# A two-layer encoder trunk: no GpSimd work on tiles, full inputs kept for the seven-product sums, and seven products in the first feed-forward layer from its eleventh tile on

## The chip, the cores and the metric

The kernel runs on one core of one Trainium2 chip. The core has TensorE (PE, matrix products; PEld is its weight loads), VectorE (DVE), ScalarE (ACT), GpSimd (POOL) and SyncE (SP), which here issues every transfer. The metric is the device time of one launch in microseconds. Before the change it is 2225.82 us, the median of three runs (2225.81 to 2229.15).

## The reference

512 tokens of width 1024 pass two layers of three residual blocks. Each block's input is modulated by a condition vector c, and each block ends in a layer norm:

```
for i in range(2):
    mods = (silu(c) @ ada_w[i] + ada_b[i]).reshape(b, 3, 3, 1024)      # shift, scale, gate of each block
    y = swiglu(modulate(x, mods[:, 0]), w_gate, w_up, w_down)          # width 2816
    x = layer_norm(ALPHA * x + 0.5 * gate(0) * y, g, b)
    u = modulate(x, mods[:, 1])
    y = mamba2_bidir(u, ...) if i == 0 else diff_attention(u, ...)
    x = layer_norm(ALPHA * x + gate(1) * y, g, b)
    y = swiglu(modulate(x, mods[:, 2]), w_gate, w_up, w_down)
    x = layer_norm(ALPHA * x + 0.5 * gate(2) * y, g, b)
def swiglu(u, w_gate, w_up, w_down): return (silu(u @ w_gate) * (u @ w_up)) @ w_down
```

All of it is float32. A modulation by `mods` follows each layer norm, so the kernel folds the two into one scale and one bias per channel.

## The kernel before

Activations lie transposed: 1024 channels are eight tiles (KT) of 128 partitions by 512 tokens. The residual `res` holds eight such tiles for the whole run. A float32 product is made from rounded high and low parts, with three matmuls (`mm3`, L158 to L166: high-high, high-low, low-high). A weight block of 512 KB lands in a ring of four `raw` buffers; ScalarE rounds it to its high part (L119 `wh`) and VectorE subtracts to get the low part (L120 `wl`). The first blocks of each stage go into tiles of the activation pool instead, in halves of 512 columns (`wah` L110, `wal` L112), and every first half's low part is made by GpSimd.

The stages by number n are: 0 feed-forward, 1 state-space mixer, 2 and 3 feed-forward, 4 attention, 5 feed-forward. Each ends in a layer norm LN0 to LN5. In the profiled execution they lie roughly so: FFN0 from 11 to 352 us, LN0 to 405, mixer to 806, LN1 to 850, FFN2 to 1166, LN2 to 1213, FFN3 to 1533, LN3 to 1573, attention to 1829, LN4 to 1866, FFN5 to 2178, LN5 to 2226.

A feed-forward stage (`ffn`, L507) runs 22 pairs of gate and up tiles in parts of 8, 7 and 7, and after each part its down projection, eight units (`down_units`) of one 128-channel output tile each. A standard pair takes 2 x 24 matmuls of 512 columns. From tile `first7` on a pair is made by `seven` (L476): seven products of half-size blocks instead of eight, with sums of weight blocks (`weight_forms`, L454 to L464) and sums of input halves (`input_forms`, L424), which are made over the four tiles before `first7`. FFN2, FFN3 and FFN5 have `first7=4`; FFN0 has 22, so it has no such tile, though its forms are made at tiles 18 to 21.

The modulation vectors are a product of weights with the condition, made by VectorE from blocks of 512 KB (`ada_unit`, L180). `ada_stream` is a list of such units; `advance(stream, k)` puts k of them into the program at that place. `per` says how many: its first number for a standard tile, its second for a unit of the down projection of parts 0 and 1. FFN0 has (3, 0), FFN2 and FFN3 (1, 2).

The last down projection of a stage holds the layer norm. Its first units run on all 512 tokens, the last ones (four, in some stages six) on each half of the tokens in turn, so that the first half's statistics can be made while the second half is computed. `LN.start` subtracts the channel-tile mean (L272 matmul, L274 copy, L277 eight subtractions, of which GpSimd does the last two). `feed` adds up the values (`sc`, L292) and their squares (`ss`, L293), on GpSimd except at the end. `stats` makes the mean and variance with matmuls (L299, L303), takes the power on GpSimd (L317), and spreads it by matmuls (L249). `normalize` multiplies (L347), writes the next input's high part `uh` and a temporary full-precision copy `lt` with ScalarE (L349), and the low part `ul` with VectorE (L350). L371 adds a down-projection result to the residual.

The order of instructions on each engine is fixed when the kernel is built: a scheduler places them by program order, by readiness and by when tiles of the pools come free. Tiles with the tag `a` (the activation pool: `hi`, `lo`, `wah`, `wal` and others) share NA = 32 buffers, and are handed out in the order of the program's requests.

Of the kernel before, what the change touches and what calls it, by code (L numbers as in the profile page):

```python
# [9 lines left out]
F32 = mybir.dt.float32  # L10
F32R = mybir.dt.float32r
AF = mybir.ActivationFunctionType
# [5 lines left out]
KT = D // P  # L18
FT = 22
FPARTS = (8, 7, 7)  # L20
NA = 32
NE = 5
NG = 4
NST = 128
# [22 lines left out]
def hybrid_trunk(tc, xT, cb, par, cst, adaw, wgu, wdn0, wdn1, wdn2, wdt, win, wso, wqk, wv, wao, dist_in, dtp, lam_in, out):  # L47
# [17 lines left out]
    def tmp(name="tmp"):  # L65
        return tp.tile([P, T], F32, tag="t", name=name)
# [28 lines left out]

    extra = [None]
    behind = []
    first_split = [True]
    first_ln = [None]
    turn = [0]  # L100

    def split(raw, where=None):

        n = raw.shape[-1]
        if where == "a":
            hi, lo = [], []
            for o in range(0, n, T):
                r = raw[:, o : o + T]
                h, l = big(F32R, "wah"), big(F32R, "wal")
                x = nc.scalar.activation(h, r, AF.Copy)  # L110
                eng = nc.vector if first_split[0] or o else nc.gpsimd
                y = eng.tensor_tensor(out=l, in0=r, in1=h.bitcast(F32), op=ALU.subtract)  # L112
                for a, b in zip((x, y), behind):
                    tc.add_manual_dep(a.ins, b.ins.name, NOSYNC, reason="inputs before weights")
                hi.append(h)
                lo.append(l)
            return [(hi[c // T][:, c % T : c % T + P], lo[c // T][:, c % T : c % T + P]) for c in range(0, n, P)]
        hi, lo = ring()
        nc.scalar.activation(hi[:, :n], raw, AF.Copy)  # L119
        nc.vector.tensor_tensor(out=lo[:, :n], in0=raw, in1=hi[:, :n].bitcast(F32), op=ALU.subtract)  # L120
        return Unit(hi, lo, n)
# [138 lines left out]
    class LN:  # L260
# [6 lines left out]
        def start(self):  # L267

            pm = acc("ln")
            z0 = tp.tile([P, T], F32R, tag="t", name="z0")  # L270
            nc.scalar.activation(z0, res[0], AF.Copy)
            nc.tensor.matmul(pm, lhsT=onesn, rhs=z0, start=True, stop=True)  # L272
            m0 = ap.tile([P, T], F32, tag="l", name="m0", bufs=3)
            nc.scalar.activation(m0, pm, AF.Copy)  # L274
            for d in range(KT):
                eng = nc.gpsimd if d >= 6 else nc.vector
                eng.tensor_tensor(out=res[d], in0=res[d], in1=m0, op=ALU.subtract)  # L277
# [3 lines left out]
        def feed(self, d, a, b, late=False):  # L281
# [11 lines left out]
            e1.tensor_tensor(out=self.ss[:, a:b], in0=self.ss[:, a:b], in1=sq[:, a:b], op=ALU.add)  # L293

        def stats(self, a, b):
            n, m = self.n, (b - a) // P
# [27 lines left out]
        def normalize(self, a, b, rb):  # L324
# [14 lines left out]
            if self.u is None:  # L339
                self.u = [  # L340
                    tuple(ap.tile([P, T], F32R, tag="u", name=x, bufs=2 * KT) for x in ("uh", "ul")) for _ in range(KT)
                ]
            for d in range(KT):
                G, B = lnG[n][:, d : d + 1], lnB[n][:, d : d + 1]
                z, t = res[d][:, a:b], tmp("lt")[:, a:b]
                uh, ul = self.u[d][0][:, a:b], self.u[d][1][:, a:b]
                nc.vector.tensor_tensor(out=z, in0=z, in1=rb, op=ALU.mult)  # L347
                for o in (uh, t):
                    nc.scalar.activation(o, z, AF.Identity, bias=B, scale=G)  # L349
                nc.vector.tensor_tensor(out=ul, in0=t, in1=uh.bitcast(F32), op=ALU.subtract)  # L350
# [22 lines left out]
            op0=ALU.mult, op1=ALU.add,  # L373
        )

    next_u = [None]

    def first_units(n):

# [8 lines left out]
    def down_units(n, u, units, last, KEEP=4):  # L388
# [15 lines left out]
        if last:  # L404
            rbs = []
            for a, b in HALVES:
                for d, w in keep:
                    pd = acc()
                    proj(pd, w, u, cols=((a, b),))
                    add_res(d, pd, n, a, b)  # L410
                    ln.feed(d, a, b, late=True)
# [11 lines left out]

    def input_forms(u):

        for k in range(4):
            top, bot = tmp("ft"), tmp("fb")
            for o, d in ((top, k), (bot, k + 4)):  # L430
                nc.vector.tensor_tensor(out=o, in0=u[d][0].bitcast(F32), in1=u[d][1].bitcast(F32), op=ALU.add)
# [72 lines left out]
        hs.append(split_act(sg))  # L504


    def ffn(n, stream=None, per=(0, 0), pre=None, first7=FT):  # L507
# [6 lines left out]
        u = next_u[0]  # L514
        f = 0
        pre = pre or first_units(n)
        for pi, nf in enumerate(FPARTS):
            hs = []
            open7 = None
            for _ in range(nf):  # L520
# [19 lines left out]
                nc.vector.tensor_tensor(out=h, in0=sg, in1=pu, op=ALU.mult)  # L540
                hs.append(split_act(h))
                if first7 - 4 <= f < first7:
                    making = making or input_forms(u)
# [490 lines left out]
    for d in range(KT):  # L1034
# [20 lines left out]
    first_split[0] = False  # L1055
# [114 lines left out]
```

## Time and profile before

| what | value |
|---|---|
| median of 3 runs | 2225.82 us (2225.81 to 2229.15) |
| profiled execution | 2227.95 us, span 2226.2 us |
| granted TensorE clock, mean | 0.991 |
| PE busy | 2161.8 us (97%) |
| DVE busy | 1697.3 us (76%) |
| ACT busy | 1055.2 us (47%) |
| POOL busy | 273.4 us (12%) |
| read from memory | 289.5 MB |

Busy times are of one execution. In a row of a group the count follows the x, then come busy time and mean duration in ns; the last column says how long the engine stood idle before and what released it. Where a row has three durations with slashes they are the shortest, the median and the longest, and the two times behind them are the first and the last start. In the rows of the timeline the first number is the start and the second the duration in us. A matmul's duration is longer than the distance to the next one, since matmuls overlap.

### The profile page before, as it was taken

Reading aid. Unit: us, or ns where it says so; the run is one execution under the profiler, and the core shown is the slowest. Engines: PE = TensorE matmul, PEld = TensorE weight load, DVE = VectorE, ACT = ScalarE, POOL = GpSimd, SP = SyncE. Lnnn points to the kernel's source line nnn. Section 1 sums busy time; section 2 is a strip of 40 time slices with the busy share of each in tenths; the row PEclk is TensorE's granted clock in tenths of the full one; section 3 lists DMA queues with packets and bytes.
Section 4 is the critical chain, followed back from the end, with each engine's and each line's share of the span. In section 5 each row is a group of like instructions: output and inputs, shape, how many; then the busy total and the mean of one; then the engine's idle time right before and its main releaser. Section 6 shows DMA issues by size and latency. Waiting matters only on the chain.

```text
span 2226.2 us, 33653 instructions
## 1 busy us (share of the span) xinstructions
PE 2161.8 (97%) x13030; PEld 1862.6 (84%) x13030; DVE 1697.3 (76%) x2850; ACT 1055.2 (47%) x1758; POOL 273.4 (12%) x332
## 2 busy tenths in 40 slices
PE   7999999999999989999999999999999999999998
PEld 5788888866777679889898989899877778989897
DVE  6865568556766689989888998897766679959696
ACT  4422234757656537434355534344755556425253
POOL 2000003035332330000003000003000012000003
PEclk9999999999999999999999999999999999999999
DMA  8865562375445423545542273733211122323231
GB/s 300 283 210 175 181 200 80 96 184 150 136 132 156 119 70 107 193 156 184 166 133 92 92 253 103 238 106 122 68 57 52 53 67 67 115 75 116 84 117 46
DMA packets 88545, 296.97 MB, mean 133 GB/s; under 512 B 9536, under 2 KB 12992, under 8 KB 88384
## 3 DMA queue, kind: packets, MB, share of 16 engines
q1 hardware_dynamic: 88384, 294.81, 41.8%
q8 instruction: 102, 1.67, 0.3%
q14 instruction: 59, 0.48, 0.1%
HBM read 289.53 MB, written 5.24 MB: 132 GB/s over the span
## 4 chain that ended last, share of the span: by engine, by line
PE 48%; DVE 9%; issue 4%; ACT 3%; DMA 2%; POOL 1%; POOLq 0%; ACTq 0%; DVEq 0%; SPq 0%
PE acc L162 38%; PE mid L162 6%; DVE wl L120 1%; DMA raw<-in_wdn 1%; PE mid L938 1%; DVE raw L464 1%; PE ln L162 1%; DVE wl L455 1%; DVE raw L180 1%; DVE lo L150 1%; PE ln L249 1%; DMA raw<-in_adaw 1%; ACT wh L119 1%; DVE resid L277 1%; DVE resid L371 0%
## 5 line engine op out<-in xcount | busy, mean ns | idle before, releaser
L162 PE MATMUL acc<-hi,wh 128*128 128x512 f32 (+1 forms) x1488 | 506.0, 341 | 9.8 <-DVE resid L371 6.7
L162 PE MATMUL acc<-hi,wl 128*128 128x512 f32 (+1 forms) x1488 | 505.9, 340 | 1.1 <-DVE wl L455 1.1
L162 PE MATMUL acc<-lo,wh 128*128 128x512 f32 (+1 forms) x1488 | 504.9, 339 | 0.0
L162 PE MATMUL acc<-uh,wh 128*128 128x512 f32 (+1 forms) x1256 | 441.6, 352 | 0.3 <-ACT wh L119 0.3
L162 PE MATMUL acc<-ul,wh 128*128 128x512 f32 (+1 forms) x1256 | 439.5, 350 | 0.2 <-DVE ul L1047 0.2
L162 PE MATMUL acc<-uh,wl 128*128 128x512 f32 (+1 forms) x1256 | 438.2, 349 | 0.8 <-DVE wl L120 0.8
L119 ACT ACTIVATE wh<-raw 128x1024 fp32r<-128x1024 f32 (+1 forms) x234 | 238.6, 1025 | 392.3 <-PE acc L162 199.1
L120 DVE TENSOR_TENSOR wl<-raw,wh 128x1024 fp32r<-128x1024 f32 (+1 forms) x234 | 281.2, 1202 | 81.1 <-ACT wh L119 71.3
L162 PEld LDWEIGHTS acc<-hi,wh 128*128 128x128 f32 x1488 | 283.8, 191 | 46.2 <-DVE resid L371 6.5
L162 PEld LDWEIGHTS acc<-hi,wl 128*128 128x128 f32 x1488 | 284.1, 191 | 32.2 <-DVE wl L455 1.5
L162 PEld LDWEIGHTS acc<-lo,wh 128*128 128x128 f32 x1488 | 283.9, 191 | 31.0 <-DVE lo L150 1.0
L162 PEld LDWEIGHTS acc<-uh,wh 128*128 128x128 f32 x1256 | 237.4, 189 | 40.2 <-issue 9.2
L454 ACT ACTIVATE wh<-raw 128x1024 fp32r<-128x1024 f32 x162 | 170.8, 1059 | 207.5 <-DVE raw L464 105.2
L162 PEld LDWEIGHTS acc<-uh,wl 128*128 128x128 f32 x1256 | 237.6, 189 | 35.0 <-issue 3.9
L162 PEld LDWEIGHTS acc<-ul,wh 128*128 128x128 f32 x1256 | 237.8, 189 | 33.7 <-issue 4.4
L180 DVE SCALAR_TENSOR_TENSOR raw<-raw,cond 128x1024 f32<-128x1024 f32 x144 | 176.9, 1235 | 55.8 <-DMA raw<-in_adaw 55.4
L455 DVE TENSOR_TENSOR wl<-raw,wh 128x1024 fp32r<-128x1024 f32 x162 | 196.9, 1219 | 27.1 <-ACT wh L454 26.1
L371 DVE SCALAR_TENSOR_TENSOR resid<-acc,gv,resid 128x512 f32<-128x512 f32 (+1 forms) x172 | 113.0, 659 | 78.5 <-PE acc L162 78.2
L464 DVE TENSOR_TENSOR raw<-raw 128x512 f32<-128x512 f32 x216 | 148.1, 689 | 4.4
L112 POOL TENSOR_TENSOR wal<-raw,wah 128x512 fp32r<-128x512 f32 x13 | 19.7, 1517 | 951.7 <-ACT wah L110 655.5
L162 PE MATMUL mid<-uh,wh 128*128 128x256 f32 (+2 forms) x332 | 94.7, 286 | 0.9 <-DVE up L496 0.9
L162 PE MATMUL mid<-uh,wl 128*128 128x256 f32 (+2 forms) x332 | 93.9, 283 | 0.0
(269 smaller groups left out, 3824.8 us busy)
## 6 DMA issues: line engine op xcount, KB each, us to landing
raw<-in_wgu SPq DMA_DIRECT2D x176, 512.0 KB, 3.9
raw<-in_adaw SPq DMA_DIRECT2D x144, 512.0 KB, 4.6
raw<-in_wdn SPq DMA_DIRECT2D x64, 448.0 KB, 3.7
raw<-in_win SPq DMA_DIRECT2D x40, 512.0 KB, 3.6
raw<-in_wdn SPq DMA_DIRECT2D x32, 512.0 KB, 4.5
rw<-scr SPq DMA_DIRECT2D x32, 512.0 KB, 5.4
ch<-scr SPq DMA_DIRECT2D x32, 256.0 KB, 3.5
raw<-in_wso SPq DMA_DIRECT2D x16, 512.0 KB, 3.5
```

The source lines that it names most:

```text
L119: nc.scalar.activation(hi[:, :n], raw, AF.Copy)
L120: nc.vector.tensor_tensor(out=lo[:, :n], in0=raw, in1=hi[:, :n].bitcast(F32), op=ALU.subtract)
L150: y = nc.vector.tensor_tensor(out=lo, in0=src, in1=hi.bitcast(F32), op=ALU.subtract)
L162: last = nc.tensor.matmul(o, lhsT=a, rhs=b, start=start and j == 0, stop=j == n - 1, skip_group_check=not start)
L180: nc.vector.scalar_tensor_tensor(out=raw, in0=raw, scalar=1.0, in1=cond, op0=ALU.mult, op1=ALU.mult, accum_out=mods[l][:, j : j + 1],)
L249: nc.tensor.matmul(o[:, j * P : (j + 1) * P], lhsT=cols[:, j : j + 1].broadcast_to([P, P]), rhs=ident, start=True, stop=True)
L277: eng.tensor_tensor(out=res[d], in0=res[d], in1=m0, op=ALU.subtract)
L371: nc.vector.scalar_tensor_tensor(out=res[d][:, a:b], in0=pd[:, a:b], scalar=gvec[n][:, d : d + 1], in1=res[d][:, a:b], op0=ALU.mult, op1=A ...
L454: nc.scalar.activation(x[0], r, AF.Copy)
L455: nc.vector.tensor_tensor(out=x[1], in0=r, in1=x[0].bitcast(F32), op=ALU.subtract)
L464: nc.vector.tensor_tensor(out=o, in0=x, in1=y, op=ALU.add)
L938: nc.tensor.matmul(ss[m], lhsT=a[r, c], rhs=b[r, :], start=j == 0, stop=j == 2)
```

## The change

Three things change. GpSimd's arithmetic on whole tiles goes to VectorE (the low parts of weights, the mean subtractions, the sums of the layer norms, the first low input) and the first scaling of the residual by ALPHA goes to ScalarE, put into the list `later`. GpSimd keeps the powers, masks, and the mixer's decay additions. In LN1, LN2 and LN4, `normalize` writes its full-precision copy into eight kept tiles `uf` of the activation pool (NA is 35 now), and `input_forms` of the next feed-forward stage reads those, where it added high and low part before. (LN1 feeds FFN2, LN2 feeds FFN3, LN4 feeds FFN5.) In FFN0 `first7` is 10, so tiles 10 to 21 use seven products, and `per` has three numbers: two modulation units for a standard tile, two for a down unit of parts 0 and 1, one for a down unit of part 2.

```diff
-NA = 32
+NA = 35
@@ split
-                eng = nc.vector if first_split[0] or o else nc.gpsimd
-                y = eng.tensor_tensor(out=l, in0=r, in1=h.bitcast(F32), op=ALU.subtract)
+                y = nc.vector.tensor_tensor(out=l, in0=r, in1=h.bitcast(F32), op=ALU.subtract)
@@ LN.start
-                eng = nc.gpsimd if d >= 6 else nc.vector
-                eng.tensor_tensor(out=res[d], in0=res[d], in1=m0, op=ALU.subtract)
+                nc.vector.tensor_tensor(out=res[d], in0=res[d], in1=m0, op=ALU.subtract)
@@ LN.feed
-            e0 = nc.vector if late else nc.gpsimd
-            e1 = nc.vector if late and d == KT - 1 else nc.gpsimd
-            e0.tensor_tensor(out=self.sc[:, a:b], in0=c0[:, a:b], in1=z, op=ALU.add)
-            e1.tensor_tensor(out=self.ss[:, a:b], in0=self.ss[:, a:b], in1=sq[:, a:b], op=ALU.add)
+            nc.vector.tensor_tensor(out=self.sc[:, a:b], in0=c0[:, a:b], in1=z, op=ALU.add)
+            nc.vector.tensor_tensor(out=self.ss[:, a:b], in0=self.ss[:, a:b], in1=sq[:, a:b], op=ALU.add)
@@ LN.normalize
+            if a == 0:
+                keep = n in (1, 2, 4)
+                self.full = [big(name="uf") if keep else None for _ in range(KT)]
+                next_full[0] = self.full if keep else None
...
-                z, t = res[d][:, a:b], tmp("lt")[:, a:b]
+                z, t = res[d][:, a:b], (self.full[d] or tmp("lt"))[:, a:b]
@@ input_forms
-            top, bot = tmp("ft"), tmp("fb")
-            for o, d in ((top, k), (bot, k + 4)):
-                nc.vector.tensor_tensor(out=o, in0=u[d][0].bitcast(F32), in1=u[d][1].bitcast(F32), op=ALU.add)
+            if full is not None:
+                top, bot = full[k], full[k + 4]
+            else:
+                top, bot = tmp("ft"), tmp("fb")
+                for o, d in ((top, k), (bot, k + 4)):
+                    nc.vector.tensor_tensor(out=o, in0=u[d][0].bitcast(F32), in1=u[d][1].bitcast(F32), op=ALU.add)
@@ ffn
-                if pi < 2:
-                    advance(stream, per[1])
+                advance(stream, per[1 if pi < 2 else 2])
@@ start of the program
-        eng = nc.gpsimd if d == 0 else nc.vector
-        y = eng.tensor_tensor(out=hl[1], in0=uf, in1=hl[0].bitcast(F32), op=ALU.subtract)
+        y = nc.vector.tensor_tensor(out=hl[1], in0=uf, in1=hl[0].bitcast(F32), op=ALU.subtract)
-        nc.gpsimd.tensor_scalar(out=res[d], in0=res[d], scalar1=ALPHA, scalar2=None, op0=ALU.mult)
+        later.append(lambda d=d: nc.scalar.activation(res[d], res[d], AF.Copy, scale=ALPHA))
-    ffn(0, st0, (3, 0), [[k[j] for k in ks] for j in range(8)])
+    ffn(0, st0, (2, 2, 1), [[k[j] for k in ks] for j in range(8)], first7=10)
-    ffn(2, st1, (1, 2), first7=4)
-    ffn(3, st1, (1, 2), first7=4)
+    ffn(2, st1, (1, 2, 0), first7=4)
+    ffn(3, st1, (1, 2, 0), first7=4)
```

More of the change, by code (lines that the diff above doesn't have):

```diff
@@ L97, in hybrid_trunk @@
     behind = []
-    first_split = [True]
     first_ln = [None]
@@ L275, in start, with feed @@
             for d in range(KT):
-                eng = nc.gpsimd if d >= 6 else nc.vector
-                eng.tensor_tensor(out=res[d], in0=res[d], in1=m0, op=ALU.subtract)
+                nc.vector.tensor_tensor(out=res[d], in0=res[d], in1=m0, op=ALU.subtract)
             self.sc = ap.tile([P, T], F32, tag="l", name="sc", bufs=3)
             self.ss = ap.tile([P, T], F32, tag="l", name="ss", bufs=3)
-        def feed(self, d, a, b, late=False):
+        def feed(self, d, a, b):
             z = res[d][:, a:b]
@@ L374, in add_res @@
         )
-    next_u = [None]
+    next_u, next_full = [None], [None]
     def first_units(n):
@@ L410, in down_units @@
                     add_res(d, pd, n, a, b)
-                    ln.feed(d, a, b, late=True)
+                    ln.feed(d, a, b)
                 if rbs:
@@ L417, in down_units, with input_forms @@
             ln.residual()
-    def input_forms(u):
+    def input_forms(u, full):
         for k in range(4):
-            top, bot = tmp("ft"), tmp("fb")
-            for o, d in ((top, k), (bot, k + 4)):
-                nc.vector.tensor_tensor(out=o, in0=u[d][0].bitcast(F32), in1=u[d][1].bitcast(F32), op=ALU.add)
+            if full is not None:
[4 more added lines that the diff above has]
+                    nc.vector.tensor_tensor(out=o, in0=u[d][0].bitcast(F32), in1=u[d][1].bitcast(F32), op=ALU.add)
             t5, t7, t4, t2 = top[:, :H], top[:, H:], bot[:, :H], bot[:, H:]
@@ L504, in seven, with ffn @@
         hs.append(split_act(sg))
-    def ffn(n, stream=None, per=(0, 0), pre=None, first7=FT):
+    def ffn(n, stream=None, per=(0, 0, 0), pre=None, first7=FT):
         forms, making = [], None
@@ L513, in ffn @@
         idx = {0: 0, 2: 1, 3: 2, 5: 3}[n]
-        u = next_u[0]
+        u, full = next_u[0], next_full[0]
         f = 0
@@ L542, in ffn @@
                 if first7 - 4 <= f < first7:
-                    making = making or input_forms(u)
+                    making = making or input_forms(u, full)
                     forms.append(next(making))
@@ L1054, in hybrid_trunk @@
     nc.sync.dma_start(csts, cst[:, : 2 * P].rearrange("p (j q) -> p j q", j=2))
-    first_split[0] = False
     behind.clear()
```

## The prediction

> **What bounds the kernel now.** I read the page first, then busy time by stretch, then the places where TensorE (PE) stands still, and last what it waits for there.
>
> ```profile
> span 2226.2 us, 33653 instructions
> PE 2161.8 (97%) x13030; PEld 1862.6 (84%) x13030; DVE 1697.3 (76%) x2850; ACT 1055.2 (47%) x1758; POOL 273.4 (12%) x332
> ```
>
> PE is busy 97% of the span, so nearly everywhere a change is worth what it takes from or gives to PE's stream. GpSimd (POOL) is busy 12% and bounds nothing by itself. The profiled execution took 2227.95 us; the median is 2225.82, 2.1 below it. The sum is made against 2227.95 and the 2.1 is taken off at the end. Busy time by stretch (one row each; PEclk is the granted clock):
>
> ```profile
> core 0: us, PE busy (x) PEld busy (x) DVE busy (x) ACT busy (x) POOL busy (x), PEclk, DMA share, GB/s
> 157.00:200.00 43.00, 43.00 (x188) 35.16 (x188) 28.02 (x39) 12.68 (x16) 0.00 (x0) 1.00 0.71 230
> 1100.00:1150.00 50.00, 50.00 (x421) 49.87 (x420) 47.41 (x73) 25.93 (x40) 0.00 (x0) 1.00 0.37 112
> 1020.00:1058.00 38.00, 35.59 (x254) 32.80 (x254) 34.34 (x59) 14.25 (x24) 0.00 (x0) 1.00 0.67 220
> 1385.00:1425.00 40.00, 36.98 (x264) 34.02 (x263) 35.87 (x62) 15.08 (x24) 0.00 (x0) 1.00 0.68 216
> 806.00:837.00 31.00, 26.48 (x175) 24.78 (x173) 26.71 (x48) 11.40 (x22) 17.78 (x17) 0.89 0.25 84
> 836.00:859.00 23.00, 21.62 (x168) 20.41 (x167) 19.73 (x55) 20.72 (x40) 1.64 (x2) 1.00 0.26 89
> 1829.00:1857.00 28.00, 22.70 (x164) 21.60 (x163) 24.70 (x46) 12.33 (x21) 16.22 (x15) 0.94 0.26 86
> 1166.00:1200.00 34.00, 29.52 (x172) 26.49 (x171) 30.61 (x42) 9.66 (x16) 20.00 (x14) 0.91 0.44 140
> ```
>
> The first row is the first feed-forward layer in the tiles that change: PE full, VectorE (DVE) 28 of 43 us. The second is seven-product tiles in a later layer: PE full, DVE 47.41 of 50. Rows three and four are down projections after seven-product tiles, with two modulation blocks per unit: PE idle 2.4 and 3.0 us. Rows five, seven and eight are the down-projection ends of the layers before LN1, LN4 and LN2, where GpSimd is at work: PE idle 4.5 of 31, 5.3 of 28, 4.5 of 34, with the clock granted 0.89 to 0.94. Row six is LN1's tail: PE is almost full.
>
> **Part 1: seven products, −12.8.** A standard tile's period from one SiLU (L538) to the next, and that of a seven-product tile from the chain of waits:
>
> ```profile
> 158.22 0.58 ACT L538 ACTIVATE sg<-acc 128x512 f32<-128x512 f32 x1
> ...
> 191.41 0.58 ACT L538 ACTIVATE sg<-acc 128x512 f32<-128x512 f32 x1
> 1132.27 7.15 PE acc L162 x60
> 1142.25 7.13 PE acc L162 x60
> 1152.26 5.87 PE acc L162 x43
> ```
>
> (191.41 − 158.22) / 3 is 11.06 us, (1152.26 − 1132.27) / 2 is 10.0: a difference of 1.07. Twelve tiles (10 to 21): −12.8. The input forms were made in this layer before too, so they add nothing. Bounds: 0, if DVE (47.41 of 50 busy, the nearest row) fails to keep up, and −12.8. These tiles load no modulation blocks, as in the later layers, so I take −12.8.
>
> **Part 2: modulation blocks moved to the down projections, +4.3.** Before, no block was loaded there in this layer. Now two come with each unit of parts 0 and 1, as in the rows 1020:1058 and 1385:1425. Part 1 follows seven-product tiles: +3.3, between the 2.4 and 3.0 of those rows and the part of the stall that lies at their edges. Part 0 follows standard tiles: +1. Together 0 (all hidden, as in 157:200 at 230 GB/s) to 7. LN0 gets its sums on DVE, which has room there: +0.5.
>
> **Part 3: GpSimd's tile work goes to DVE; the fronts of the normalizations.** The mean subtraction shows what the two engines do to each other:
>
> ```profile
> L277 DVE TENSOR_TENSOR resid<-resid,m x36: 677/686/1786, 353.4 to 2185.3; 128x512 f32<-128x512 f32 x36
> L277 POOL TENSOR_TENSOR resid<-resid,m x12: 1422/1742/1823, 354.2 to 2181.9; 128x512 f32<-128x512 f32 x12
> 813.69 0.28 PE L162 MATMUL acc<-hi,wl 128*128 128x256 f32 x1
> 816.89 0.39 PE L162 MATMUL acc<-hi,wh 128*128 128x256 f32 x1 [2.92 <-DVE resid L371]
> 1181.15 2.28 DVE L120 TENSOR_TENSOR wl<-raw,wh 128x1024 fp32r<-128x1024 f32 x1
> L120 DVE TENSOR_TENSOR wl<-raw,wh 128x1024 fp32r<-128x1024 f32 (+1 forms) x234 | 281.2, 1202 | 81.1 <-ACT wh L119 71.3
> 1182.31 2.27 POOL L293 TENSOR_TENSOR ss<-ss,sq 128x512 f32<-128x512 f32 x1
> ```
>
> A DVE subtraction takes 0.69 us, beside GpSimd up to 1.79; at 813.69 PE waits 3.2 us for DVE's L371, queued behind six of them. Beside GpSimd's L293 a DVE weight split takes 2.28, against a mean of 1.20 over all 234. After the change DVE has all eight subtractions (about 0.61 each, end to end, 4.9) and every sum, but each at its short time. Walking along the built order, I get the first scaling of LN1 (L347 before, L346 after) 2.5 us earlier; LN4's front likewise, −1.5. LN2's front goes from L272 to L249, and LN3's is the same piece with less GpSimd overlap:
>
> ```profile
> 1166.80 0.50 PE L272 MATMUL ln<-z,onesn 128*128 128x512 f32 x1 [0.21 <-ACT z L271]
> 1199.95 0.92 PE L249 MATMUL ln<-csts,rr 128*128 128x128 f32 x4
> 1533.53 0.50 PE L272 MATMUL ln<-z,onesn 128*128 128x512 f32 x1 [0.68 <-ACT z L271]
> 1559.53 0.71 PE L249 MATMUL ln<-csts,rr 128*128 128x128 f32 x4
> ```
>
> 33.2 against 26.0: −7.2. Fronts together −11.2; at most −16 (all PE idle of the three front rows, 14.3, and the lost clock), at least −4. LN3 −0.5 and LN5 −1.0 by the same reasoning.
>
> **Part 4: the kept inputs.** They save 8 additions of 0.68 us in each of three layers:
>
> ```profile
> L431 DVE TENSOR_TENSOR fb<-uh,ul x16: 678/684/687, 315.0 to 1907.6; 128x512 f32<-128x512 f32 x16
> ```
>
> That is DVE time beside a full PE, so I give it −1.5 in all, for PE's small stalls at the first seven-product tiles of FFN2. Against it stands what the order shows: the kept tiles come from the same pool as the first weights of the next stage, and those weights are now split only after them. ScalarE's order at LN1, before:
>
> ```order
> L110 ACTIVATE wah<-raw 128x512
> L288 ACTIVATE sq<-resid 128x512
> L288 ACTIVATE sq<-resid 128x256 x5
> L119 ACTIVATE wh<-raw 128x1024
> L288 ACTIVATE sq<-resid 128x256
> L110 ACTIVATE wah<-raw 128x512 x2
> L288 ACTIVATE sq<-resid 128x256 x5
> L349 ACTIVATE uh<-resid,lnB_2254,lnG_2252 128x256
> ```
>
> and after the change (here L109 is the split, L348 the normalized input), the end of the second half:
>
> ```order
> L348 ACTIVATE uh<-resid,lnB_3275,lnG_3273 128x256
> L348 ACTIVATE uf<-resid,lnB_3275,lnG_3273 128x256
> L109 ACTIVATE wah<-raw 128x512
> L356 ACTIVATE resid<-resid,lnab_3280,lnag_3278 128x512
> L109 ACTIVATE wah<-raw 128x512
> ```
>
> All six splits stood ahead of the first normalized input. Now the first stands behind the first half's sixteen (eight uh, eight uf) and the other five, of which this is the beginning, behind the second half's sixteen. PE's order at the end of the last down-projection unit, before:
>
> ```order
> L162 MATMUL acc<-hi,wl 128x256
> L162 MATMUL acc<-uh,wah 128x256 x3
> L162 MATMUL acc<-uh,wh 128x256
> L299 MATMUL mid<-sc,onesd 128x256
> L303 MATMUL ln<-invd,sc 128x1 x2
> L303 MATMUL ln<-invd,ss 128x1 x2
> L162 MATMUL acc<-ul,wah 128x256
> ```
>
> and now (L294, L298 and L247 are the sums, statistics and broadcast):
>
> ```order
> L160 MATMUL acc<-hi,wl 128x256
> L294 MATMUL mid<-sc,onesd 128x256
> L298 MATMUL ln<-invd,sc 128x1 x2
> L298 MATMUL ln<-invd,ss 128x1 x2
> L247 MATMUL ln<-csts,rr 128x128 x2
> L160 MATMUL acc<-uh,wah 128x256
> L160 MATMUL acc<-ul,wah 128x256
> L160 MATMUL acc<-uh,wal 128x256
> ```
>
> Before, 44 projection matmuls stood between the statistics and the broadcast and PE ran on; now none does, and the third projection matmul waits for a low half. In the trace those weights were ready long before use (LN1, LN2 and LN4, in this order):
>
> ```profile
> L110 ACT ACTIVATE wah<-raw x6: 612/615/617, 800.9 to 825.1; 128x512 fp32r<-128x512 f32 x6
> L162 PE MATMUL acc<-ul,wah x48: 278/283/389, 839.4 to 858.7; 128*128 128x256 f32 x48
> L162 PE MATMUL acc<-ul,wah x48: 278/283/363, 1207.9 to 1227.0; 128*128 128x256 f32 x48
> L162 PE MATMUL acc<-ul,wah x48: 280/283/288, 1860.3 to 1878.3; 128*128 128x256 f32 x48
> 836.37 0.28 PE L162 MATMUL acc<-lo,wh 128*128 128x256 f32 x1
> 836.49 0.28 PE L162 MATMUL acc<-hi,wl 128*128 128x256 f32 x1
> 843.64 0.59 ACT L349 ACTIVATE uh<-resid,lnB,lnG 128x256 fp32r<-128x256 f32 x1
> 844.13 0.59 ACT L349 ACTIVATE lt<-resid,lnB,lnG 128x256 f32<-128x256 f32 x1
> 839.40 1.08 DVE L347 TENSOR_TENSOR resid<-resid,ln 128x256 f32<-128x256 f32 x3
> ```
>
> LN1 by the new order, counted from the last down-projection matmul (836.49 before): ScalarE writes an input every 0.49 us (843.64 to 844.13), so the first sixteen end at 7.9 and the first split (0.61) at 8.5. DVE works at about 0.335 per half tile (839.40 row: three in 1.08, overlapping); the second broadcast comes at about 7, the second half's scaling starts at 9.2, and the first low half, queued behind it, ends at about 13.3. Twelve matmuls run. ScalarE's second sixteen end at 17.1, the second split at 17.7, its low half at 18.4. The other 132 of the 144 matmuls take 0.119 each, 15.7: 34.1. Two pauses of the length that stands before a lowered clock add 1.3 us: 35.4. Before it was 858.7 − 836.49 = 22.2. **Tail of LN1: +13.2.** The same walk gives LN4 +14.1, and LN2, which has some other projection matmuls to run in between, +11.5. Bounds for each: +5 (the second broadcast and the first low half 4 us earlier each) and +15. Together +38.8, between +15 and +45. Nothing hides it: the projection's own matmuls are what used to fill it, and the next tiles queue behind them on PE.
>
> [...]
>
> **The sum.** −12.8 + 4.3 + 0.5 − 11.2 − 0.5 − 1.0 − 1.5 + 38.8 = +16.6: 2244.5 in a profiled execution, and 2242.4 for the median. I predict **2242**.
>
> **Rivals.**
> (a) The tails cost nothing, because DVE's own chain of statistics and scaling ends last there anyway and the projection matmuls only move within it. Then the sum is 16.6 − 38.8 = −22.2: 2204, faster. For it: DVE is 19.73 of 23 us busy in 836:859, so PE was not far ahead of it. Against it: PE is 21.62 of 23 busy there, with projection matmuls. 5%.
> (b) The tails cost about half (+19), since the second half's work on DVE and ScalarE overlaps better than I walk it: −3, 2223, range 2215 to 2229. From +22.2 of tails on, the change is no gain. 19%.
> (c) Seven products don't pay in the first layer, DVE being nearly full (47.41 of 50) when the two sums and weight forms meet: +12.8 on mine, 2255. Against it: three other layers run them with PE at 50.00 of 50. 12%.
> (d) My forecast, 2233 to 2252: 64%.
>
> Of the 19% of (b), 9 are faster, 7 within 0.2% (4.5 us, what a measurement of this kernel can tell from no change) and 3 slower. So faster 0.14, same 0.07, slower 0.79. The range is 2222 to 2256: (a), the lower half of (b) and the upper part of (c) are left out; the likeliest case's own range is 2233 to 2252.
>
> **What would show it.** In the changed trace: PE idle of 10 us or more between the last h,w matmul and the bulk of the uh,wah matmuls at LN1 and LN4, released by DVE wal; the first wah split at LN1 after the first uf; 144 projection matmuls done some 33 to 36 us after the last down-projection matmul. A seven-product period of 10.0 in the first layer. L277 on DVE at 0.68 throughout and no 3 us wait for L371. I am wrong if those tails are under 28 us, or if the wah splits run ahead of the uf tiles in the trace.

## The result, and the profile after

The changed kernel takes 2245.32 us in the median (four runs, 2243.26 to 2253.86) against 2227.49 us before (the three runs of the table above and a fourth, 2225.81 to 2229.16): the ratio is 1.0087, 95% interval 1.0058 to 1.0116. It is slower by 0.9%. The profiled execution's span goes from 2226.2 to 2242.1 us, 15.9 more. The page of the changed kernel:

```profile
span 2242.1 us, 34579 instructions
PE 2151.8 (96%) x13462; PEld 1875.9 (84%) x13462; DVE 1758.6 (78%) x3056; ACT 1085.5 (48%) x1814; POOL 137.3 (6%) x226
```

GpSimd's work is halved and PE is busy 10 us less, yet the span is longer: PE waits more. Where it does, seen by stretch (the first three rows are LN1's front, its tail, and the end of its tail; then front and tail of LN2, and of LN4):

```profile
core 0: us, PE busy (x) PEld busy (x) DVE busy (x) ACT busy (x) POOL busy (x), PEclk, DMA share, GB/s
793.00:816.00 23.00, 21.05 (x165) 20.26 (x164) 20.92 (x52) 6.53 (x14) 0.70 (x1) 1.00 0.11 37
816.00:837.00 21.00, 6.48 (x30) 5.25 (x29) 20.27 (x60) 18.36 (x38) 0.70 (x1) 0.61 0.08 25
837.00:855.00 18.00, 18.00 (x134) 17.73 (x135) 15.81 (x27) 15.67 (x22) 0.00 (x0) 0.88 0.78 239
1161.00:1197.00 36.00, 34.18 (x234) 31.41 (x233) 29.49 (x62) 10.32 (x20) 0.70 (x1) 1.00 0.23 73
1197.00:1232.00 35.00, 26.03 (x178) 24.90 (x176) 33.29 (x80) 30.55 (x53) 0.69 (x1) 0.80 0.42 135
1831.00:1854.20 23.20, 21.11 (x164) 20.21 (x164) 21.13 (x52) 7.50 (x15) 0.69 (x1) 1.00 0.10 35
1854.20:1892.50 38.30, 24.24 (x161) 22.76 (x160) 34.43 (x83) 34.50 (x60) 0.69 (x1) 0.73 0.31 102
```

The fronts are better: before, the three stretches showed PE idle 4.5 to 5.3 us and a clock of 0.89 to 0.94; now it is idle 2 us and the clock is full. The tails are bad. For the 21 us behind LN1's front PE runs 6.48 us. What it waits for, in PE's timeline from the last down-projection matmul on, with ScalarE's and VectorE's rows beside it:

```profile
815.99 0.28 PE L160 MATMUL acc<-hi,wl 128*128 128x256 f32 x1
818.82 0.70 PE L294 MATMUL mid<-sc,onesd 128*128 128x256 f32 x2 [2.55 <-DVE sc L287]
825.65 1.23 PE L247 MATMUL ln<-csts,rr 128*128 128x128 f32 x4 [5.35 <-POOL rr L312]
827.32 0.58 PE L160 MATMUL acc<-uh,wah 128*128 128x256 f32 x1 [0.45 <-ACT wah L109]
832.43 0.58 PE L160 MATMUL acc<-uh,wal 128*128 128x256 f32 x1 [4.31 <-DVE wal L110]
836.79 0.58 PE L160 MATMUL acc<-uh,wah 128*128 128x256 f32 x1 [1.86 <-ACT wah L109]
...
826.66 0.61 ACT L109 ACTIVATE wah<-raw 128x512 fp32r<-128x512 f32 x1
835.64 0.58 ACT L348 ACTIVATE uf<-resid,lnB,lnG 128x256 f32<-128x256 f32 x1
836.13 0.61 ACT L109 ACTIVATE wah<-raw 128x512 fp32r<-128x512 f32 x1
...
831.69 0.68 DVE L110 TENSOR_TENSOR wal<-raw,wah 128x512 fp32r<-128x512 f32 x1
836.83 0.68 DVE L110 TENSOR_TENSOR wal<-raw,wah 128x512 fp32r<-128x512 f32 x1
```

PE stands still four times: for the last sum, for the second half's power (no projection matmul is left to fill that time), for the first low half of a weight, and for the second weight half, whose high part ScalarE writes right behind the last kept tile (835.64, 836.13). Such waits come to 8.9 us at LN2 and 14.1 at LN4, against 14.5 here.

Between fixed marks in the traces (the first statistics matmul of each normalization, the last down-projection matmul, the last matmul on weights split in advance) the executions divide like this; a front lies between the first two marks, a tail between the last two:

| piece, us | before | after | e2 kept only | e4 GpSimd only | e1 not kept | e3 weights first | e7 late squares |
|---|---|---|---|---|---|---|---|
| first layer to LN0 | 352.3 | 343.1 | 351.8 | 348.5 | 345.2 | 342.6 | 344.1 |
| LN0 | 54.3 | 53.0 | 54.3 | 53.7 | 53.0 | 53.2 | 55.0 |
| mixer | 402.2 | 397.1 | 397.5 | 398.9 | 399.9 | 400.0 | 399.9 |
| LN1 front | 27.7 | 22.9 | 27.0 | 23.1 | 23.1 | 23.1 | 24.2 |
| LN1 tail | 22.3 | 38.7 | 33.4 | 29.1 | 28.3 | 25.9 | 25.0 |
| FFN2 | 308.0 | 306.4 | 308.3 | 307.2 | 305.1 | 305.9 | 304.8 |
| LN2 front | 40.8 | 35.9 | 36.6 | 33.5 | 34.2 | 38.5 | 37.0 |
| LN2 tail | 19.4 | 35.0 | 33.0 | 20.7 | 20.7 | 20.7 | 19.3 |
| FFN3 | 306.5 | 303.4 | 307.6 | 303.8 | 304.2 | 306.0 | 304.0 |
| LN4 front | 26.7 | 23.2 | 28.1 | 23.0 | 23.0 | 23.0 | 24.3 |
| LN4 tail | 21.7 | 38.3 | 37.5 | 26.2 | 26.2 | 24.6 | 22.3 |
| all the rest | 644.3 | 645.2 | 643.9 | 644.1 | 644.6 | 644.6 | 643.7 |
| span | 2226.2 | 2242.1 | 2259.1 | 2211.7 | 2207.3 | 2208.0 | 2203.6 |

From before to after: first layer −9.2, LN0 −1.3, mixer −5.1, FFN2 and FFN3 −4.7, the three fronts −13.2, the three tails +48.5, the rest +0.9. Their sum is the 15.9.

### The profile page after: what moved, and what is told of

Its sections match the earlier page's. It is cut to its first block, busy times and chain, and to the rows that moved or that the text cites. A ratio compares the mean times of both kernels' runs of the same rounds, so it can differ in the third digit from the quotient of the medians.

```text
span 2242.1 us, 34579 instructions
## 1 busy us (share of the span) xinstructions
PE 2151.8 (96%) x13462; PEld 1875.9 (84%) x13462; DVE 1758.6 (78%) x3056; ACT 1085.5 (48%) x1814; POOL 137.3 (6%) x226
## 4 chain that ended last, share of the span: by engine, by line
PE 50%; DVE 9%; ACT 3%; DMA 3%; issue 2%; POOL 1%; POOLq 0%; ACTq 0%; DVEq 0%; SPq 0%
PE acc L160 40%; PE mid L160 6%; DVE raw L467 1%; PE mid L940 1%; DMA raw<-in_wdn 1%; DVE wl L118 1%; DMA raw<-in_adaw 1%; PE ln L160 1%; DVE wl L458 1%; ACT uh L348 1%; ACT uf L348 1%; DVE raw L178 1%; DVE resid L274 1%; PE ln L247 1%; PE ln L962 0%
## 5 line engine op out<-in xcount | busy, mean ns | idle before, releaser
L160 PE MATMUL acc<-hi,wh 128*128 128x256 f32 (+1 forms) x1584 | 531.3, 336 | 7.5 <-DVE resid L370 3.9
L160 PE MATMUL acc<-hi,wl 128*128 128x256 f32 (+1 forms) x1584 | 530.2, 335 | 0.0
L160 PE MATMUL acc<-lo,wh 128*128 128x256 f32 (+1 forms) x1584 | 529.6, 335 | 0.6 <-DVE lo L148 0.6
L160 PE MATMUL acc<-uh,wh 128*128 128x256 f32 (+1 forms) x1160 | 392.6, 339 | 0.0
L160 PE MATMUL acc<-ul,wh 128*128 128x256 f32 (+1 forms) x1160 | 390.1, 336 | 0.0
L160 PE MATMUL acc<-uh,wl 128*128 128x256 f32 (+1 forms) x1160 | 388.6, 336 | 0.0
L457 ACT ACTIVATE wh<-raw 128x1024 fp32r<-128x1024 f32 x198 | 209.1, 1059 | 288.5 <-DVE raw L467 120.5
L458 DVE TENSOR_TENSOR wl<-raw,wh 128x1024 fp32r<-128x1024 f32 x198 | 240.8, 1219 | 49.2 <-ACT wh L457 48.2
L178 DVE SCALAR_TENSOR_TENSOR raw<-raw,cond 128x1024 f32<-128x1024 f32 x144 | 174.2, 1218 | 19.3 <-DMA raw<-in_adaw 19.0
L467 DVE TENSOR_TENSOR raw<-raw 128x512 f32<-128x512 f32 x264 | 180.8, 689 | 5.6
L160 PE MATMUL mid<-ul,wh 128*128 128x256 f32 (+2 forms) x380 | 108.2, 285 | 0.0
```

Source lines behind the costliest of these rows:

```text
L160: last = nc.tensor.matmul(o, lhsT=a, rhs=b, start=start and j == 0, stop=j == n - 1, skip_group_check=not start)
L178: nc.vector.scalar_tensor_tensor(out=raw, in0=raw, scalar=1.0, in1=cond, op0=ALU.mult, op1=ALU.mult, accum_out=mods[l][:, j : j + 1],)
L457: nc.scalar.activation(x[0], r, AF.Copy)
L458: nc.vector.tensor_tensor(out=x[1], in0=r, in1=x[0].bitcast(F32), op=ALU.subtract)
L467: nc.vector.tensor_tensor(out=o, in0=x, in1=y, op=ALU.add)
```

## The experiments

The ratios are against the kernel before, run beside each on the same chip. The labels e1 to e11 name the runs; pieces and waits are of one profiled execution each.

**Theory T and its rival (e1).** T: the kept tiles stand ahead of the next weights in their pool, and this makes the tails. V: VectorE has GpSimd's sums to do, and this makes the tails. The first run takes the kept tiles away from the change:

```diff
-                keep = n in (1, 2, 4)
+                keep = False
```

> The change without the kept inputs: the normalizations write the temporary copy again and the input forms make their eight additions per layer. Theory T (the kept tiles stand ahead of the next stage's first weights in their pool, so those weights are split late and PE runs dry behind LN1, LN2 and LN4): the three tails, counted from the last down-projection matmul to the last matmul on the split weights, fall from 38.7, 35.0 and 38.3 us to about 22.3, 19.4 and 21.7 as before, 48 us less; about 2 us come back for the additions, so about 2199 us. Rival V (the tails are long because VectorE has GpSimd's sums to do there): tails stay above 33 us, about 2245.

2206.62 us, ratio 0.9928 (0.9913 to 0.9944): without the kept inputs the same kernel is 0.7% faster than before, where it was 0.9% slower. The tails fall by 10.5, 14.3 and 12.1 us, 36.8 together, and not by 48. LN2's is nearly back; LN1's and LN4's stay 6.0 and 4.5 us above before. So the kept tiles make three quarters of it (T). The other 11.7 us are there without them; how much of those the sums make (V) is taken up with e7.

**The kept tiles alone (e2)**, on the kernel before (GpSimd as it was, no new seven-product tiles, 35 buffers, the edits of `normalize` and `input_forms` from the change):

> The kernel before with the kept inputs alone (35 buffers, eight kept tiles in LN1, LN2 and LN4); GpSimd works as before and the first layer has no seven-product tiles. Theory T: the three tails get as long as in the change, 35 to 39 us, so about 2227 + 45 = 2272 us, less about 2 for the additions that go: 2270. Rival V: GpSimd has its sums here, so the tails stay near 20 to 24 us and the time near 2226.

2260.37 us, ratio 1.0171 (1.0156 to 1.0186). V alone would have had this one at no change. The tails grow by 11.1, 13.6 and 15.8 us, with the same order in time, here at LN1 (all six high halves stand behind the first kept tiles):

```profile
L110 ACT ACTIVATE wah<-raw x6: 612/614/623, 839.3 to 854.0; 128x512 fp32r<-128x512 f32 x6
L162 PE MATMUL acc<-ul,wah x48: 278/283/415, 840.3 to 864.0; 128*128 128x256 f32 x48
```

Before, the six stood at 800.9 to 825.1. T is confirmed. The time lies 10 below the expectation: the kernel before is at 2223.04 on this chip and not at 2227, the tails grew by 40.5 and not 45, and LN2's front, which no longer holds those splits, is 4 us shorter than before.

**The kept tiles, but the weights asked for first (e3):**

```diff
                 if rbs:
+                    if n in (1, 2, 4):
+                        next_pre[0] = first_units(n + 1)
                     ln.normalize(*HALVES[0], rbs[0])
...
-        pre = pre or first_units(n)
+        pre = pre or next_pre[0] or first_units(n)
+        next_pre[0] = None
```

> The change, with one thing moved: at LN1, LN2 and LN4 the next stage's three first weight blocks are asked for ahead of the kept tiles, so that their twelve halves come first in the pool. Theory T: tails of 20 to 24 us as before with the kept inputs still in use, about 48 us less than the change: 2197 us. Rival V: above 2240. A third way: the twelve halves and eight kept tiles do not fit at once beside the fourteen high and low parts of the last part's inputs, the kept tiles wait instead, and the tails stay 30 us or more, 2220 to 2245.

2209.05 us, ratio 0.9944 (0.9926 to 0.9961). One request moved takes away nearly all of the loss:

```profile
L109 ACT ACTIVATE wah<-raw x6: 613/616/621, 787.9 to 821.2; 128x512 fp32r<-128x512 f32 x6
L348 ACT ACTIVATE uf<-resid,lnB,lnG x16: 584/586/589, 824.2 to 840.2; 128x256 f32<-128x256 f32 x16
L160 PE MATMUL acc<-ul,wah x48: 278/283/583, 825.3 to 844.6; 128*128 128x256 f32 x48
```

It did not reach the 2197 expected: the tails of LN1 and LN4 stay 3.6 and 2.9 us above before, and LN2's front is 4 us longer than without kept tiles. The splits are not why: both fronts hold the same four low halves. VectorE waits 2.1 us there for a modulation block from memory (0.6 in e1), PE 2.0 for the sum behind it, and the granted clock over the front is 0.91 (1.00 in e1). The third way, that twenty tiles don't fit, is out. Beside the run without kept tiles this one shows what keeping buys: FFN2 305.9 against 305.1, FFN3 306.0 against 304.2, FFN5 300.5 against 300.6. It is nothing here.

**GpSimd's work moved, and nothing else (e4):**

```diff
-NA = 35
+NA = 32
-                keep = n in (1, 2, 4)
+                keep = False
-    ffn(0, st0, (2, 2, 1), [[k[j] for k in ks] for j in range(8)], first7=10)
+    ffn(0, st0, (3, 0, 0), [[k[j] for k in ks] for j in range(8)])
```

> The kernel before with GpSimd's arithmetic on whole tiles moved to VectorE and the first scaling to ScalarE, nothing else (32 buffers, no kept inputs, no seven-product tiles in the first layer, three modulation blocks per standard tile). By the change's trace the start of the first layer is 5.4 us shorter and the fronts of LN1, LN2 and LN4 together 13.2 us: about 2208 us if tails are as before (theory T). Rival V: the tails get long here too, 35 us and more, about 2250. If the shorter start came from the modulation blocks that were moved and not from GpSimd, the start is as before and the time about 2213.

2214.26 us, ratio 0.9968 (0.9950 to 0.9985). The fronts are as short as in the change or shorter (23.1, 33.5, 23.0), so their gain comes from GpSimd. The tails of LN1 and LN4 are 6.8 and 4.5 us longer than before without any kept tile: V again. The start is between the two cases: it is 3.8 us shorter, and with it the first layer, so some of the 9.2 is GpSimd's. The time is near the 2213 of the third case, but not for its reason. The mean subtraction in the changed kernel, where GpSimd is out of the way, answers the row of before (677/686/1786):

```profile
L274 DVE TENSOR_TENSOR resid<-resid,m x48: 680/684/692, 345.5 to 2199.3; 128x512 f32<-128x512 f32 x48
```

**Seven products in the first layer, and nothing else (e5)** (the two edits of `ffn` and its call on the kernel before):

> The kernel before with seven-product tiles from the eleventh tile of the first layer and the modulation blocks moved to its down projections, nothing else. By my sum: 12.8 us less for the tiles, 4.3 back for the blocks: 8.5 us less, about 2216 on this chip. In the change's trace PE loses 5.8 us to pauses between the first down projection's end and LN0's start, and 0.8 in the first down projection: 6.2 us less, about 2218. If the start (5.4 us shorter in the change) owes its gain to the moved blocks rather than to GpSimd, 10 us less, about 2214.

2225.04 us, ratio 1.0005 (0.9994 to 1.0016): no change, where I expected 6 to 10 us. The first layer does get 5.9 us shorter, to 346.4. LN0's front takes it back, 40.2 against 34.4. Its windows, this run and the kernel before, and then PE's longest wait in this run's:

```profile
346.00:380.00 34.00, 30.03 (x177) 27.27 (x177) 29.88 (x45) 9.34 (x17) 21.35 (x15) 0.91 0.45 146
```

```profile
352.00:386.00 34.00, 34.00 (x231) 31.22 (x231) 27.47 (x49) 13.03 (x26) 20.65 (x17) 1.00 0.26 83
```

```profile
PE mid L299 <- DVE sc L292: 2.6, 1, 2.6
```

Modulation blocks now come with the units of the last down projection, where VectorE is slower beside GpSimd: in this run a block's product (L180) takes 1.99, 1.68 and 2.30 us between 348 and 361 us, behind GpSimd's first subtraction at 347.6, against 1.23 at 343.80. PE waits 2.6 us for a sum and the granted clock over the window is 0.91, as it was in LN2 before. It takes both: LN0's front is 34.4 us before, 34.4 with GpSimd's work moved and no blocks there (e4), 33.7 with both moved (e1), and 40.2 with the blocks beside GpSimd. With GpSimd's work moved the same edit pays: e1 is 4.4 us shorter in span than e4, and its LN0 is no longer (53.0 against 53.7). So the seven products need GpSimd's part of the change; that part pays without them (e4).

**The modulation blocks of the first layer's down projections left out (e6)** (no load, no product; a zero is written in the column's place):

```diff
     def ada_unit(l, j):
+        if leave_out[0]:
+            nc.vector.memset(mods[l][:, j : j + 1], 0.0)
+            return
...
+                leave_out[0] = n == 0
                 advance(stream, per[1 if pi < 2 else 2])
+                leave_out[0] = False
```

> The change without the kept inputs, and with the 40 modulation blocks in the first layer's down projections left out: not loaded, not multiplied, their columns set to zero (so the gates, shifts and scales that come from them are left out of the result). If these blocks cause PE's pauses in the seven-product parts (theory B: VectorE and the queue of loads are late by them), the layer from the first down projection's end to LN0's start takes 190 us or less instead of 196 to 198, and the mean of its seven-product period stays at 10.0. If the pauses come from the passage between seven-product tiles and plain units itself (rival P: the last tile's SiLU and split stand in the way whatever is loaded), it stays above 194.

One execution: 2202.36 us. The layer from the end of the first down projection (146.9) to LN0 (337.9) takes 191.0 us, a little above the 190 of theory B and well under rival P's 194. PE over the same 196 us, in the change and here:

```profile
147.00:343.00 196.00, 192.80 (x1312) 176.91 (x1310) 176.23 (x278) 82.50 (x120) 0.00 (x0) 1.00 0.50 164
```

```profile
147.00:343.00 196.00, 196.00 (x1332) 180.46 (x1331) 150.81 (x228) 82.84 (x121) 0.00 (x0) 1.00 0.34 107
```

PE's pauses are gone with the blocks, and with them 25 us of VectorE's work, so theory B holds. Load and product were left out together; which of the two makes PE late is not shown.

**The late squares' sums on GpSimd again (e7)**, without kept tiles, to test V where it acts. In the kernel before, the values' sums in these halves were VectorE's already, and the squares' sums GpSimd's up to the last tile:

```diff
-        def feed(self, d, a, b):
+        def feed(self, d, a, b, late=False):
...
-            nc.vector.tensor_tensor(out=self.ss[:, a:b], in0=self.ss[:, a:b], in1=sq[:, a:b], op=ALU.add)
+            e1 = nc.gpsimd if late and d < KT - 1 else nc.vector
+            e1.tensor_tensor(out=self.ss[:, a:b], in0=self.ss[:, a:b], in1=sq[:, a:b], op=ALU.add)
```

> The change without the kept inputs, and with the squares' sums in the halves of the last units on GpSimd again, as in the kernel before (six or ten half-tile additions per half). In that kernel without them the tails of LN1 and LN4 are 28.3 and 26.2 us against 22.3 and 21.7 before. If VectorE's sums behind the last matmul make this difference, the tails come back to 22 to 24 us and the fronts stay at 23 to 25: about 6 to 8 us less than without, if GpSimd's beside VectorE's additions cost little. If the two engines slow each other as in the kernel before (0.58 against 0.41 us for a sum), the fronts of LN1 and LN4 grow by 2 to 4 us and nothing is won.

2204.95 us, ratio 0.9913 (0.9895 to 0.9931). The tails come back to 25.0, 19.3 and 22.3, against 28.3, 20.7 and 26.2. PE's wait for the last sum of LN1, behind the last down-projection matmul, goes with them (e1, then e7):

```profile
823.81 0.70 PE L294 MATMUL mid<-sc,onesd 128*128 128x256 f32 x2 [2.45 <-DVE sc L287]
```

```profile
825.28 0.70 PE L295 MATMUL mid<-sc,onesd 128*128 128x256 f32 x2 [0.28 <-DVE sc L287]
```

V is confirmed as the smaller cause, for 8.6 of the 11.7 us; 2.7 us stay at LN1 and 0.6 at LN4. The fronts pay with 1.1, 2.9 and 1.3 us, and in a second profile of the same kernel (e10 below) with 1.2, 4.5 and 1.3. The time hardly moves against e1 (0.9913 against 0.9928, with intervals that overlap).

**Other places for the blocks (e8):** three per standard tile and one per unit of every down projection.

```diff
-    ffn(0, st0, (2, 2, 1), [[k[j] for k in ks] for j in range(8)], first7=10)
+    ffn(0, st0, (3, 1, 1), [[k[j] for k in ks] for j in range(8)], first7=10)
```

> The change without the kept inputs, with three modulation blocks per standard tile and one per unit of every down projection in the first layer (two, two and one there). If the blocks in the units cost the pauses, these fall from some 6 to 3 us; seven standard tiles carry seven more blocks, and the start, whose transfer engines are busy 0.8 to 0.9, loses 0 to 4 us; the eleven blocks left over follow at the end and cost up to 13 us of VectorE time beside the mixer's first products. I expect no change within 3 us: 2204 to 2210.

2232.75 us, ratio 1.0040 (1.0024 to 1.0057). I had the leftover blocks at up to 13 us beside other work; they cost 22, all in LN0's tail (41.7 us against 19.3). PE's waits there, and the mixer's first weight halves in this run, then in the run without kept tiles:

```profile
PE acc L160 <- ACT wah L109: 14.8, 1, 14.8
...
L109 ACT ACTIVATE wah<-raw x4: 612/622/632, 399.6 to 403.4; 128x512 fp32r<-128x512 f32 x4
```

```profile
L109 ACT ACTIVATE wah<-raw x4: 615/616/632, 352.7 to 364.2; 128x512 fp32r<-128x512 f32 x4
```

The leftover blocks stand ahead of those weights (`in_win`) in the order of loads, which all go through the ring of four buffers:

```profile
346.39 47.60 SPq L93 DMA_DIRECT2D raw<-in_adaw  x10
395.14 2.15 SPq L93 DMA_DIRECT2D raw<-in_win  x2
```

The weights' halves come 39 to 47 us later than they did. It is theory T's mechanism in another pool.

**Better versions.** Two causes of long tails were suspected without the kept tiles: low halves made behind the second half's inputs, and the sums. The first is taken away at LN1 and LN4 by asking for the weights early (e9, `n in (1, 4)` in the edit above), the second by the late squares (e10, the kernel of e7 again), and both together (e11):

> The change without the kept inputs, and with the next stage's three first weight blocks asked for ahead of the first half's normalized inputs at LN1 and LN4 (not at LN2, where the run with the weights first had a front of 38.5 us against 34.2). In the run without the kept inputs three of the six low halves at LN1 are still made behind the second half's inputs. If that costs PE, the tails of LN1 and LN4 fall from 28.3 and 26.2 to about 25.9 and 24.6, as with the weights first: 4 us less, about 2203. If not, 2206.

> The change without the kept inputs and with the late squares' sums on GpSimd, as in the run of that name, timed again beside the others: its parts gave 3.7 us less span than without GpSimd. 2203 to 2206 and faster than the kernel before by 0.7 to 1.0%.

> Both: weights asked for early at LN1 and LN4, and the late squares' sums on GpSimd. If the two causes of long tails add up (low halves made late, VectorE's sums behind the last matmul), the tails of LN1 and LN4 fall below 24 and 22 us, and the time to about 2200. If early weights push VectorE's work into the fronts, these grow by as much, and the time stays at 2203 to 2206.

| run | us | ratio (interval) | LN1 tail | LN4 tail | span |
|---|---|---|---|---|---|
| weights early | 2206.32 | 0.9911 (0.9895 to 0.9926) | 26.0 | 24.1 | 2198.6 |
| late squares, again | 2203.54 | 0.9902 (0.9888 to 0.9915) | 25.0 | 22.3 | 2204.9 |
| both | 2203.11 | 0.9900 (0.9886 to 0.9915) | 25.2 | 22.2 | 2199.1 |

The weights asked for early give the 2 us per tail that were expected, but no time against e1 (0.9911 and 0.9928), and with the late squares nothing more at LN1 and LN4: the two causes don't add up. The fronts of e11 did not grow either (24.3 and 24.4 us, against 24.3 twice in e10), so the second reading that I had for that case is not shown; why stays open. All three are about 1% faster than the kernel before, and by their ratios some 1.8% faster than the changed one; the times don't tell them apart.

## Why the prediction was right, point by point

I predicted 2242 us with a range of 2222 to 2256 and the likeliest case at 2233 to 2252; it is 2245.32. The cause that carried the forecast, part 4, is what the runs show. Its size and some other terms were off and made up for each other, so that the sum came so near (+16.6 forecast, 15.9 by the spans, 17.8 by the medians) is partly luck:

| term | forecast, us | measured in the change |
|---|---|---|
| seven products and moved blocks, first layer | −12.8 + 4.3 = −8.5 | −9.2 |
| LN0 | +0.5 | −1.3 |
| fronts of LN1, LN2, LN4 | −2.5 − 7.2 − 1.5 = −11.2 | −4.8 − 5.0 − 3.4 = −13.2 |
| tails of LN1, LN2, LN4 | +13.2 + 11.5 + 14.1 = +38.8 | +16.4 + 15.5 + 16.6 = +48.5 |
| FFN2 | −1.5 | −1.6 |
| not in the sum: mixer, FFN3 | 0 | −5.1, −3.1 |
| the rest, with LN3 and LN5 | −1.5 | +0.9 |

**The tails.** The walk along the built order had PE's waits for the power and for the weights' halves in their places, and was short by 3.3 us at LN1 (38.7 against 35.4). The first step of it failed: it let the first normalized input begin with the last down-projection matmul, as before (836.55 and 836.49). VectorE still had sums to do there (PE waits 2.55 us for the last), and ScalarE's first write came 2.8 us behind that matmul (815.99). Before, then after:

```profile
836.55 0.60 ACT L349 ACTIVATE uh<-resid,lnB,lnG 128x256 fp32r<-128x256 f32 x1 [0.19 <-DVE resid L347]
```

```profile
818.79 0.58 ACT L348 ACTIVATE uh<-resid,lnB,lnG 128x256 fp32r<-128x256 f32 x1
```

From then on every mark is late by some 3 us: the first low half ends at 16.4 us behind the matmul (walk: 13.3), the second at 21.5 (18.4). From there to the last matmul it is 17.2 us, where the walk had 15.7 and 1.3 for the clock, so that last stretch came out near. No run shows the 1.3 us for two pauses by itself; it was my estimate: in the change LN1's pauses (1.9 to 5.3 us) ran into one slow stretch, with the granted clock at 0.50 from 822 to 840 us. At LN4 the tail is 2.4 us and at LN2 4.0 us above the forecast; the walk for these two is not written out, so which of its steps failed there stays open. The upper bound of +45 was too small for the same reason: I had put all of VectorE's extra work into the fronts. The runs split the 48.5 into 36.8 that go with the kept tiles (40.5 when they are added alone, e2), close to the 38.8, and 11.7 that come with GpSimd's move, 8.6 of them from the squares' sums; no term of mine held those. Of the signs that I had named, two failed: 144 projection matmuls done after 33 to 36 us (38.7 at LN1 and 38.3 at LN4), and 10 us of idle PE released by low halves of weights. PE was idle 14.5 us at LN1, but low halves released only 4.3 of them, and the power was the longest single wait with 5.3.

**The fronts.** GpSimd's slowing was the right cause: with its work moved alone (e4) they are 4.6, 7.3 and 3.7 us shorter. For LN2 that is the 7.2 of the forecast, and its front is then as long as LN3's (33.5), the model that I took. In the change it is 5.0, since VectorE waits there for a modulation block, and PE for the sum behind it. The change, then PE in e4:

```profile
1184.39 1.23 DVE L178 SCALAR_TENSOR_TENSOR raw<-raw,cond 128x1024 f32<-128x1024 f32 x1 [2.17 <-DMA raw<-in_adaw]
1186.54 0.70 PE L294 MATMUL mid<-sc,onesd 128*128 128x256 f32 x2 [1.79 <-DVE sc L287]
```

```profile
1184.03 0.70 PE L294 MATMUL mid<-sc,onesd 128*128 128x256 f32 x2
```

LN3 has no such blocks, so the model could not show this wait.

**The first layer.** −9.2 against −8.5 hides two errors. The start up to the first down projection is 5.4 us shorter, which I had not priced (3.8 in e4, 1.7 in e5). From the end of that projection to LN0, 196.1 us stand against 200.8, a gain of 4.7 where my terms had 12.8 − 3.3 = 9.5. (The +1 for part 0 is right: its down projection is 0.9 us longer.) The pace of the new tiles was right:

```profile
276.28 0.42 ACT L505 ACTIVATE sg<-px 128x256 f32<-128x256 f32 x1 [0.32 <-DVE px L504]
...
316.46 0.42 ACT L505 ACTIVATE sg<-px 128x256 f32<-128x256 f32 x1
327.89 0.42 ACT L505 ACTIVATE sg<-px 128x256 f32<-128x256 f32 x1 [2.00 <-DVE px L504]
```

Four periods in 40.18 us are 10.05 each. The next is 11.43, at the passage to the last down projection: the blocks of part 2's units come there, and I had given that part no price at all. e6 shows the blocks to be the cause: without them this period is 9.31, and the gain from the first down projection's end to LN0 is 9.8. That is still 3.0 short of the 12.8; the rest stays open.

**The kept inputs' gain.** I gave the additions −1.5 us. FFN2 is 1.6 shorter in the change, but in e1, which makes the additions, it is shorter still (2.9), and with the kept tiles alone (e2) it is no shorter. The forecast number was met and its reason was wrong. FFN3's 3.1 is not settled: e4 has 2.7, but e5, where nothing of the change reaches that layer, has 1.4.

**The mixer** is 5.1 us shorter in the change with PE's order unaltered. In e2, which has nothing else that reaches the mixer, it is 4.7 us shorter too. A lowered clock at its start, which the profile of before has and these two have not, is most of it (before, after, e2, at the same place of the program within 0.6 us):

```profile
406.00:436.00 30.00, 29.57 (x178) 26.32 (x177) 15.81 (x27) 19.46 (x30) 0.00 (x0) 0.89 0.27 82
```

```profile
396.00:426.00 30.00, 29.61 (x190) 26.41 (x189) 17.04 (x28) 21.23 (x31) 0.00 (x0) 1.00 0.31 90
```

```profile
406.00:436.00 30.00, 29.61 (x190) 26.38 (x189) 17.16 (x28) 21.24 (x31) 0.00 (x0) 1.00 0.31 91
```

By the 200th matmul behind LN0 the kernel before is 3.4 us late. So it is not the change's; the forecast's total was helped by it. In these three rows the same matmuls show 0.89 once and 1.00 twice; what made the difference is not shown.

**The rivals.** (a), no cost from the tails, and (b), half of it, fell with the first profile. (c), seven products that don't pay, was wrong for the change (e1 against e4) but true of that part alone (e5), by a mechanism that I had not named: not VectorE in the tiles but VectorE in the normalization behind them.

## What to carry to other kernels

When a scheduler hands out the buffers of a pool in the order of requests, a new long-lived tile also moves everything that is requested behind it. Read the built order at the places where one stage's weights are prepared under another's end; here one request put ahead of another was worth 1.4% of the time (1.0087 against 0.9944). And work that bounds nothing (GpSimd at 12%, 8 additions beside a full PE) is priced by what it delays or frees at the narrow places, so parts of a change can be worth nothing alone and something together.

## What the runs showed of the hardware that was not expected

Behind LN1 in the change the granted clock was 0.61 over 21 us with 30 PE matmul records (mean of 816 to 837), and it was still 0.88 over the 18 full us that followed. It was 0.50 from 825 to 828 us, although PE was busy 1.90 of those 3 us, and still 0.50 from 837 to 840, with PE busy all 3.00; then 0.80 from 840 to 843, and 1.00 from there to 855. The 132 matmuls behind the last pause took 17.9 us, where my walk had 15.7 for them before its 1.3 for the clock.

In e7 GpSimd's 256-column sums beside VectorE's cost about what they gain. It makes 44 of them over the six normalizations, at 791 ns in the mean. Against e1 the fronts of LN1, LN2 and LN4 are 5.3 us longer together (7.0 in the second profile), LN0 is 2.0 longer, and the three tails are 8.6 shorter. All of GpSimd's tile work in the kernel before cost these three fronts 15.7 us (before against e4).
